# A decoder block on one Trainium2 core: every large product by tokens, turned back through DVE and DRAM

## The chip, the cores and the metric

The kernel runs on one core of a Trainium2 chip. TensorE (PE) multiplies matrices and writes PSUM; VectorE (DVE) and ScalarE (ACT) do elementwise work; GpSimd is called POOL in the profile, and SyncE (SP) issues most of the DMAs. The metric is device time in microseconds for one execution, lower is better. Before the change it was 2222.48 us (median of three runs, 2220.45 to 2222.61).

## What is computed

One layer of a decoder block on 256 tokens of width 2048, in float32:

```python
h = h + 0.5 * swiglu(rms_norm(h, ffn1_norm), ffn1_w_gate, ffn1_w_up, ffn1_w_down)   # 2048 -> 5632 -> 2048
n = rms_norm(h, mix_norm)
rq, rk, rv, rg, sq, sk, sv = split(n @ w_in)
ret = silu(rg) * groupnorm(retention(rope(rq), rope(rk), rv))     # 8 heads of 128
swa = sliding_window_attention(rope(sq), rope(sk), sv, sinks)     # 16 heads of 64, window 128
h = h + concat(ret, swa) @ w_out
h = h + cross_attention(rms_norm(h, xa_norm), rms_norm(mem, mem_norm), xa_wq, xa_wkv, xa_wo)
h = h + 0.5 * swiglu(rms_norm(h, ffn2_norm), ffn2_w_gate, ffn2_w_up, ffn2_w_down)
return rms_norm(h, final_norm)
```

## The kernel before

**Operands in two parts.** Every large product is made in a float32 form of the PE that takes operands as a high and a low part: `halves` (L70) copies the high part on ACT and subtracts it on DVE to get the low part. Three matmuls, high by high, high by low and low by high, add up to one product. Weights come in pieces of 128x1024 floats, two pieces (1 MB) a DMA on SP's queue, into three buffers `wf`; `split` (L163) makes `wh` and `wl` from each, with four buffers of each. A piece is one **step** of the program: 12 matmuls of 512 columns.

**Two forms of product.** `by_tokens` (L224) holds the activations still and streams 512 columns of weights; the result stands with tokens on the partitions. `by_weights` (L235) holds a 128x128 piece of the weights still and streams the activations: one matmul of 512 columns takes high and low parts of all 256 tokens side by side (L243), one of 256 columns adds the low part of the weights (L251). Its result is turned, with features on the partitions, as the next product wants its input. The gate and up products, the sliding-window, value and gate projections, `xa_wv` and the last down product go by tokens; the first down product, the rotary queries and keys (`w_in_rqk`), `w_out`, `xa_wk`, `xa_wq` and `xa_wo` go by weights (`turned=True`).

**The stream.** `run_stream` (L188) goes through the steps of all `Unit`s in one list. At each step it first runs the small tasks that are due (`later(n, f)` puts f n steps ahead), then emits the split of the piece three steps ahead (`LOOKAHEAD`), then the step's matmuls. When a unit's last step is out, its `done` reads the accumulator. The first 16 steps alternate between the first gate and the first up product. `pin` (L176) fixes program order for the first 16 steps; after them the framework's scheduler sets each engine's order.

**Turning what went by tokens.** The product of gate and up has its tokens on the partitions and must be turned. `up_done` (L446) multiplies on DVE and transposes 32x32 squares on DVE (L453) into a tile `box`; `move` (L459) brings the squares to their partitions by 16 DMAs of 32 KB from SBUF to SBUF on SP's queue, and `made` splits the result seven steps after the product. The stream h is kept turned (`hT`); before the last down product `turn_h` (L886) turns it to tokens by 32 transposes on PE (L892).

**Norms.** `Norm.block` multiplies a block of h by its gains in two parts, `Norm.stat` adds the squares up, `finish` takes the power on POOL (L376). The gains of a norm are in `blocks`, the scale per token is applied behind the product.

Of the kernel before, what the change touches and what calls it, by code (L numbers as in the profile page):

```python
# [17 lines left out]
P = 128  # L18
# [13 lines left out]
WARM = 12  # L32
FIRST = 16
SWA_EVERY = 5
# [3 lines left out]
def decoder_block(ctx: ExitStack, tc: tile.TileContext, a: dict, out: bass.AP):  # L38
# [5 lines left out]
    small = ctx.enter_context(tc.tile_pool(name="small", bufs=8))  # L44
    ps_acc = ctx.enter_context(tc.tile_pool(name="ps_acc", bufs=2, space=bass.MemoryType.PSUM))
# [36 lines left out]

    nc.scalar.dma_start(gains, a["gains"])
# [8 lines left out]

# [36 lines left out]
    class Unit:  # L129
# [4 lines left out]
        def __init__(self, w, index, n, lhs, done, blocks, turned=False, per_half=False, pair=False):  # L134
            self.w, self.n, self.lhs, self.done = w[2 * index : 2 * index + 2] if pair else w[index], n, lhs, done
            self.blocks, self.turned, self.per_half, self.pair = list(blocks), turned, per_half, pair
            units.append(self)
# [10 lines left out]

    def load(w, piece, count):
# [4 lines left out]
    def load_pair(w, piece, cuts=(0, 1024)):  # L154

        wf = wpool.tile([P, 2, 1024], F32, tag="wf", name=nm("wf"), bufs=3)
        src = w[:, piece].rearrange("f p n -> p f n")
        for lo, hi in zip(cuts, cuts[1:]):
            nc.sync.dma_start(wf[:, :, lo:hi], src[:, :, lo:hi])
# [3 lines left out]
    def split(wf, n, parts):  # L163
        wh, wl = (wpool.tile([P, 1024], F32R, tag=x, name=nm(x)) for x in ("wh", "wl"))
        if len(wf.shape) == 4:
            dst = [x.rearrange("p (k f n) -> p k f n", k=2, f=2) for x in (wh, wl)]
            for i in range(parts):
                ks = slice(i * 2 // parts, (i + 1) * 2 // parts)
                halves(dst[0][:, ks], dst[1][:, ks], wf[:, ks])
        else:  # L170
# [5 lines left out]
    def pin():  # L176

        prev = {}
        for ins in nc.cur_bb.bb.instructions:
            if ins.engine in prev:  # L180
# [7 lines left out]
    def run_stream():  # L188
        steps = [x for u in units for x in u.steps()]
        steps[:FIRST] = [x for y in zip(steps[: FIRST // 2], steps[FIRST // 2 : FIRST]) for x in y]  # L190
        loaded = []
        for i in range(0, FIRST, 4):
            cuts = (0, 512, 1024) if i == 0 else (0, 1024)
            for lo, hi in zip(cuts, cuts[1:]):
                load_x(i // 4, lo // S, hi // S)
                if i == 0:
                    if lo == 0:
                        wf = wpool.tile([P, 2, 1024], F32, tag="wf", name=nm("wf"), bufs=3)
                        src = steps[0][0].w[:, steps[0][3]].rearrange("f p n -> p f n")
                    nc.sync.dma_start(wf[:, :, lo:hi], src[:, :, lo:hi])  # L200
            if i == 0:
                v = wf.rearrange("p f (k n) -> p k f n", n=S)
                both = [[v[:, 2 * j : 2 * j + 2] for j in range(2)]]
            else:
                both = [load_pair(steps[i][0].w, steps[i][3])]
            both.append(load_pair(steps[i + 1][0].w, steps[i + 1][3]))
# [4 lines left out]
        def prepare(upto):  # L211
            while nxt[0] < min(upto, len(steps)):
# [8 lines left out]
                ready[at] = split(loaded[at], steps[at][0].n, 2 if at == 0 else 1)  # L221
# [10 lines left out]

        wide_first = [True]

        def by_weights(acc, x, wh, wl, first, last):  # L235

            wide = first or (wide_first[0] and not last)
            wide_first[0] = not wide

            def main_pass(closing):  # L240
                for k in range(4):
                    for f in range(2):
                        nc.tensor.matmul(  # L243
                            acc[:, f, :], wh[:, k, f * P : (f + 1) * P], x[:, k, :, :],
                            start=first and k == 0, stop=closing and k == 3,
                        )

            def low_pass():
                for k in range(4):
                    for f in range(2):  # L250
                        nc.tensor.matmul(  # L251
                            acc[:, f, :S], wl[:, k, f * P : (f + 1) * P], x[:, k, 0, :], start=False, stop=False
                        )
            if wide:
                main_pass(False)
                low_pass()
            else:
                low_pass()
                main_pass(last)

        held = []
        for at, (u, b, ks, _, first, last) in enumerate(steps):
# [16 lines left out]
            if u.turned:  # L279
                by_weights(u.acc[0], x, wh, wl, first, last)  # L280
# [16 lines left out]
        run_until(lambda: not tasks)  # L297

# [30 lines left out]
    class Norm:  # L329
# [12 lines left out]
        def block(self, b, src):  # L342

            x = blk()
            k = 0
# [3 lines left out]
            self.blocks[b] = x  # L349
# [44 lines left out]
        def scale_turned(self, x):  # L394
# [4 lines left out]
    def total(acc):  # L399

        x = t2k().rearrange("p (f s) -> p f s", f=2)
        copy(x, acc[:, :, S:])
        nc.vector.tensor_tensor(x, acc[:, :, :S], x, ALU.add)  # L403
        return x
# [8 lines left out]
    def add_to_h(j, acc, factor):  # L413

        v = hT[j // 2][:, 2 * (j % 2) : 2 * (j % 2) + 2, :]
        x = t2k().rearrange("p (f s) -> p f s", f=2)
        copy(x, acc[:, :, S:], scale=factor)
        nc.vector.tensor_tensor(v, v, x, ALU.add)  # L418
        nc.vector.scalar_tensor_tensor(v, acc[:, :, :S], factor, v, ALU.mult, ALU.add)  # L419

    def to_h(w, lhs, factor, blocks, norm=None, then=None):

        def done(acc, j):
            add_to_h(j, acc, factor)
            if norm is not None and j % 2 == 1:
# [610 lines left out]
```

## Time and profile before

| | |
|---|---|
| profiled execution | 2222.29 us |
| its span in the trace | 2220.5 us |
| mean granted PE clock | 0.997 |
| DMA | 427.04 MB, 192 GB/s on average |
| POOL | 17 instructions, no DMA |

The page gives the busy time of each engine as a share of the span; groups of instructions (line, engine, operation, what it writes and reads, count, busy time, mean of one, idle time before it and who ended it); the chain of work that ended last; and the DMAs with the time from issue to landing. The matmuls of PE are pipelined and their ends are modelled, so the spacing of their starts is what counts. Under 20 us of the span are outside PE's matmuls before the first and behind the last of the products: the first product's matmul starts at 7.60 us, and the last stores are issued from 2209.8 us on.

### The profile page before, as it was taken

Reading aid. Unit: us, or ns where it says so; the run is one execution under the profiler, and the core shown is the slowest. Engines: PE = TensorE matmul, PEld = TensorE weight load, DVE = VectorE, ACT = ScalarE, POOL = GpSimd, SP = SyncE. Lnnn points to the kernel's source line nnn. Section 1 sums busy time; section 2 is a strip of 40 time slices with the busy share of each in tenths; the row PEclk is TensorE's granted clock in tenths of the full one; section 3 lists DMA queues with packets and bytes.
Section 4 is the critical chain, followed back from the end, with each engine's and each line's share of the span. In section 5 each row is a group of like instructions: output and inputs, shape, how many; then the busy total and the mean of one; then the engine's idle time right before and its main releaser. Section 6 shows DMA issues by size and latency. Waiting matters only on the chain.

```text
span 2220.5 us, 27264 instructions
## 1 busy us (share of the span) xinstructions
PE 2199.1 (99%) x10898; PEld 1865.5 (84%) x10898; DVE 1290.8 (58%) x1540; ACT 1035.7 (47%) x1281; POOL 10.3 (0%) x17
## 2 busy tenths in 40 slices
PE   8999999999999999999999999999999999999998
PEld 7788888888888888888888889888888888888886
DVE  5555555455456678886765656664555554555554
ACT  5444434444445565555544554454444433444443
POOL 0000000000000000000000000000000000000000
PEclk9999999999999999999999999999999999999999
DMA  6556555565565554445555544454665565466563
GB/s 241 199 196 224 205 190 181 191 213 185 202 222 197 182 178 163 153 170 190 209 185 191 193 171 152 154 190 163 226 206 186 214 211 195 161 234 208 200 230 133
DMA packets 126527, 427.04 MB, mean 192 GB/s; under 512 B 12608, under 2 KB 23872, under 8 KB 126272
## 3 DMA queue, kind: packets, MB, share of 16 engines
q1 hardware_dynamic: 126256, 425.26, 55.2%
q8 instruction: 85, 1.39, 0.2%
q14 instruction: 42, 0.34, 0.0%
q10 hardware_dynamic: 144, 0.05, 0.0%
HBM read 411.62 MB, written 2.10 MB: 186 GB/s over the span
## 4 chain that ended last, share of the span: by engine, by line
PE 96%; SPq 1%; DMA 1%; DVE 1%; issue 1%; ACT 0%; ACTq 0%; POOLq 0%; POOL 0%
PE acc L410 21%; PE acc L409 21%; PE acc L408 21%; PE acc L243 20%; PE acc L251 10%; SPq L462 1%; DMA wf<-in_ffn_w_up 1%; PE tmp L408 0%; PE tmp L410 0%; PE tmp L409 0%; PE tmp L568 0%; DVE wl L73 0%; PE tmp L594 0%; ACT wh L68 0%; PE tmp L371 0%
## 5 line engine op out<-in xcount | busy, mean ns | idle before, releaser
L73 DVE TENSOR_TENSOR wl<-wf,wh 128x1024 fp32r<-128x1024 f32 (+1 forms) x773 | 936.8, 1221 | 721.0 <-ACT wh L68 715.0
L68 ACT ACTIVATE wh<-wf 128x1024 fp32r<-128x1024 f32 (+1 forms) x773 | 813.2, 1059 | 913.0 <-PE acc L410 609.7
L408 PE MATMUL acc<-wh,blk 128*128 128x512 f32 (+1 forms) x2112 | 821.0, 389 | 4.8 <-ACT wh L68 3.1
L409 PE MATMUL acc<-wl,blk 128*128 128x512 f32 (+1 forms) x2112 | 819.6, 388 | 2.2 <-DVE wl L73 2.2
L410 PE MATMUL acc<-wh,blk 128*128 128x512 f32 (+1 forms) x2112 | 819.4, 388 | 0.1
L243 PE MATMUL acc<-blk,wh 128*128 128x512 f32 x1984 | 480.8, 392 | 0.6 <-ACT wh L68 0.6
L408 PEld LDWEIGHTS acc<-wh,blk 128*128 128x128 f32 x2112 | 396.9, 188 | 86.1 <-ACT wh L68 3.9
L409 PEld LDWEIGHTS acc<-wl,blk 128*128 128x128 f32 x2112 | 397.1, 188 | 84.0 <-DVE wl L73 3.2
L410 PEld LDWEIGHTS acc<-wh,blk 128*128 128x128 f32 x2112 | 397.0, 188 | 81.9 <-DVE blk L327 0.5
L243 PEld LDWEIGHTS acc<-blk,wh 128*128 128x128 f32 x1984 | 364.3, 189 | 70.6 <-ACT wh L68 1.0
L251 PEld LDWEIGHTS acc<-blk,wl 128*128 128x128 f32 x1984 | 257.5, 192 | 15.1 <-ACT blk L68 4.9
L251 PE MATMUL acc<-blk,wl 128*128 128x256 f32 x1984 | 263.5, 284 | 3.8 <-ACT blk L68 3.8
L68 ACT ACTIVATE t2k<-acc 128x512 f32<-128x512 f32 x56 | 33.5, 598 | 126.0 <-PE acc L243 126.0
L418 DVE TENSOR_TENSOR h<-h,t2k 128x512 f32<-128x512 f32 x32 | 22.2, 693 | 53.7 <-ACT t2k L68 53.7
L73 DVE TENSOR_TENSOR blk<-blk,blk 128x512 fp32r<-128x512 f32 x44 | 28.5, 689 | 39.7 <-ACT blk L68 39.7
L68 ACT ACTIVATE blk<-blk 128x512 fp32r<-128x512 f32 x44 | 25.4, 625 | 52.2 <-DMA blk<-blk 52.2
L68 ACT ACTIVATE blk<-tmp 128x512 fp32r<-128x512 f32 (+3 forms) x57 | 26.0, 470 | 26.9 <-DVE blk L73 15.9
L452 DVE SCALAR_TENSOR_TENSOR t2k<-acc,n,t2k 128x512 f32<-128x512 f32 x44 | 31.1, 746 | 8.5 <-PE acc L410 8.5
L403 DVE TENSOR_TENSOR t2k<-acc,t2k 128x512 f32<-128x512 f32 x24 | 16.6, 690 | 32.9 <-ACT t2k L68 32.9
L443 ACT ACTIVATE t2k<-acc,n 128x512 f32<-128x512 f32 x44 | 27.6, 680 | 3.6 <-PE acc L410 3.3
L68 ACT ACTIVATE blk<-h,gains 128x256 fp32r<-128x256 f32 x64 | 28.2, 499 | 1.6 <-DVE h L419 1.6
L453 DVE STREAM_TRANSPOSE blk<-t2k 128x512 f32<-128x512 f32 x44 | 28.6, 686 | 0.0
(130 smaller groups left out, 612.1 us busy)
## 6 DMA issues: line engine op xcount, KB each, us to landing
wf<-in_ffn_w_up SPq DMA_DIRECT2D x88, 1024.0 KB, 5.4
wf<-in_ffn_w_gate SPq DMA_DIRECT2D x87, 1024.0 KB, 5.2
wf<-in_ffn_w_down SPq DMA_DIRECT2D x84, 1024.0 KB, 4.9
wf<-in_w_in_rqk SPq DMA_DIRECT2D x16, 1024.0 KB, 4.9
wf<-in_w_in_rvg SPq DMA_DIRECT2D x16, 1024.0 KB, 4.9
wf<-in_w_out SPq DMA_DIRECT2D x16, 1024.0 KB, 4.9
wf<-in_xa_wk SPq DMA_DIRECT2D x16, 1024.0 KB, 4.9
wf<-in_xa_wv SPq DMA_DIRECT2D x16, 1024.0 KB, 4.9
```

What stands on the lines that cost most here:

```text
L68: return nc.scalar.activation(dst, src, AF.Copy, **kw)
L73: nc.vector.tensor_tensor(lo, src, hi, ALU.subtract)
L243: nc.tensor.matmul(acc[:, f, :], wh[:, k, f * P : (f + 1) * P], x[:, k, :, :], start=first and k == 0, stop=closing and k == 3,)
L251: nc.tensor.matmul(acc[:, f, :S], wl[:, k, f * P : (f + 1) * P], x[:, k, 0, :], start=False, stop=False)
L408: nc.tensor.matmul(o, ah, bh, start=start, stop=False)
L409: nc.tensor.matmul(o, ah, bl, start=False, stop=False)
L410: nc.tensor.matmul(o, al, bh, start=False, stop=stop)
L418: nc.vector.tensor_tensor(v, v, x, ALU.add)
L443: nc.scalar.activation(gated[b][t], acc[:, t, :], AF.Silu, scale=norm.scale(t))
L452: nc.vector.scalar_tensor_tensor(s[t], acc[:, t, :], norm.scale(t), s[t], ALU.mult, ALU.mult)
L453: nc.vector.transpose(squares[:, :, :, t, :], s[t].rearrange("p (q b j) -> p q b j", q=4, b=4))
L462: nc.sync.dma_start(box[32 * j : 32 * j + 32, 1, i, :], box[32 * i : 32 * i + 32, 0, j, :])
```

## The change

All products that went by weights go by tokens, with 512 columns of weights and pairs of pieces (`pair=True`). What must be turned goes through the new function `cross`: DVE transposes the 32x32 squares of each half of the tokens into a tile `sq`; Pool's queue writes `sq` to a DRAM tile `box` (256 KB) and reads it back in four DMAs of 64 KB, each for 32 partitions, into `dst`; `TURN` = 4 steps later the task `then` uses the result. This takes the place of the SBUF moves of the FFNs, of the by-weights form, and of the PE transposes of h. `together` lays two units side by side, so that the steps on the last block of both stand behind all their others; it is used for the first two projections of the mixing stage, the first two `xa_wo` products and the first gate and up of FFN2. The first loads are cut smaller and begin with half a row block of gate, up's first half comes before gate's second, the first 128 KB of x come on ACT's queue, and 9 warming matmuls are issued in place of 12. At the end `pin` fixes program order for SP, ACT, DVE and POOL over the whole program.

```diff
-WARM = 12
+WARM = 9
+TURN = 4
...
+    nc.scalar.dma_start(hT[0][:, :1, :], a["x"][:P, :1, :])
     nc.scalar.dma_start(gains, a["gains"])
...
+    def all_steps():
+        out = []
+        rest = list(units)
+        while rest:
+            u = rest.pop(0)
+            x = u.steps()
+            if u.then is None:
+                out += x
+            else:
+                y = rest.pop(0).steps()
+                nx, ny = (sum(z[1] == s[-1][1] for z in s) for s in (x, y))
+                out += x[:-nx] + y[:-ny] + x[-nx:] + y[-ny:]
+        return out
...
+                src = [x[0].w[:, x[3]].rearrange("f p n -> p f n") for x in steps[:2]]
+                for j, lo, hi in ((0, 0, S), (0, S, 2 * S), (1, 0, 2 * S), (0, 2 * S, 1024), (1, 2 * S, 1024)):
+                    if j == 0 and lo > 0:
+                        load_x(0, lo // S, hi // S)
+                    nc.sync.dma_start(dst[j][:, :, lo:hi], src[j][:, :, lo:hi])
...
-        def by_weights(acc, x, wh, wl, first, last):
...
         run_until(lambda: not tasks)
+        pin([mybir.EngineType.SP, mybir.EngineType.Activation, mybir.EngineType.DVE, mybir.EngineType.Pool])
...
+    def cross(src, then, delay=TURN):
+        out = []
+        for v in src:
+            sq, dst = t2k(), t2k()
+            nc.vector.transpose(sq.rearrange("p (g q j) -> p q g j", g=4, q=4), v)
+            box = dram.tile([P, 512], F32, tag="box", name=nm("box"))
+            nc.gpsimd.dma_start(box, sq)
+            far = box.rearrange("(i r) (g n) -> g r i n", i=4, g=4)
+            for g in range(4):
+                nc.gpsimd.dma_start(dst[32 * g : 32 * g + 32, :].rearrange("p (i n) -> p i n", i=4), far[g])
+            out.append(dst.rearrange("p (i q j) -> p q i j", i=4, q=4))
+        later(delay, lambda: then(out))
+
+    def halves_of(out, x):
+        for t in range(2):
+            hi, lo = (x[:, :, c, t * P : (t + 1) * P].rearrange("p q (a j) -> p q a j", a=4) for c in range(2))
+            halves(hi, lo, out[t])
         return x
...
     def to_h(w, lhs, factor, blocks, norm=None, then=None):
-        def done(acc, j):
-            add_to_h(j, acc, factor)
...
-        for j in range(8):
-            Unit(w, j, 256, lhs, lambda acc, j=j: done(acc, j), blocks, turned=True)
+        def done(acc, b):
+            def add(out):
+                for t in range(2):
+                    v = hT[b][:, :, t * P : (t + 1) * P].rearrange("p q (a j) -> p q a j", a=4)
+                    nc.vector.tensor_tensor(v, v, out[t], ALU.add)
+                if norm is not None:
+                    norm.block(b, [hT[b]])
+                    norm.stat([hT[b]])
+                if then is not None:
+                    then(b)
+            s = [acc[:, t, :] for t in range(2)]
+            if factor != 1.0:
+                for t in range(2):
+                    s[t] = t2k()
+                    copy(s[t], acc[:, t, :], scale=factor)
+            cross([squares_of(x) for x in s], add)
+        for b in range(4):
+            Unit(w, b, 512, lhs, lambda acc, b=b: done(acc, b), blocks, pair=True)
...
-                for i in range(4):
-                    later(2 + i, lambda i=i: move(box, i))
-                later(7, lambda: made(b, box))
+                def made(out):
+                    acts[b] = halves_of(out, blk())
+                cross([squares_of(x) for x in s], made)
...
     def turn_h(b):
-        tp = [tmp_ps() for _ in range(2)]
-        for t in range(2):
-            for k in range(4):
-                nc.tensor.transpose(tp[t][:, k * P : (k + 1) * P], hT[b][:, k, t * P : (t + 1) * P], ident)
-            copy(h[t][:, b * 512 : (b + 1) * 512], tp[t])
+        def made(out):
+            for t in range(2):
+                copy(squares_of(h[t][:, b * 512 : (b + 1) * 512]), out[t])
+        cross([hT[b][:, :, t * P : (t + 1) * P].rearrange("p q (a j) -> p q a j", a=4) for t in range(2)], made)
```

`rqk_done` and `put_done` (rotary queries and keys; keys and queries of the cross-attention) change in the same way: what they did with the turned accumulator stands in a task of `cross`.

On DVE, behind the second up product of FFN1 (`t2k_644` and `t2k_645` are its products by gate, `wl` the low parts of weight pieces, `blk_927` the block for the down product), before:

```order
L453 STREAM_TRANSPOSE blk_787<-t2k_644 128x4x4x32
L453 STREAM_TRANSPOSE blk_787<-t2k_645 128x4x4x32
L73 TENSOR_TENSOR wl_793<-wf_769,wh_792 128x1024
L73 TENSOR_TENSOR wl_812<-wf_809,wh_811 128x1024
L73 TENSOR_TENSOR wl_832<-wf_809,wh_831 128x1024
L73 TENSOR_TENSOR wl_854<-wf_851,wh_853 128x1024
L73 TENSOR_TENSOR wl_874<-wf_851,wh_873 128x1024
L73 TENSOR_TENSOR blk_927<-blk_787,blk_927 128x4x128 x2
```

and now, at the same place (`t2k_791` and `t2k_800` are read back from DRAM):

```order
L417 STREAM_TRANSPOSE t2k_790<-t2k_645 128x4x4x32
L417 STREAM_TRANSPOSE t2k_799<-t2k_646 128x4x4x32
L75 TENSOR_TENSOR wl_809<-wf_770,wh_808 128x1024
L75 TENSOR_TENSOR wl_828<-wf_825,wh_827 128x1024
L75 TENSOR_TENSOR wl_844<-wf_825,wh_843 128x1024
L75 TENSOR_TENSOR wl_862<-wf_859,wh_861 128x1024
L75 TENSOR_TENSOR blk_877<-t2k_791,blk_877 128x4x128
L75 TENSOR_TENSOR blk_877<-t2k_800,blk_877 128x4x128
L75 TENSOR_TENSOR wl_883<-wf_859,wh_882 128x1024
```

Four splits stand between the transposes and the use of the result, where there were five; the split behind it, `wl_883`, cannot pass it.

On POOL, from the first norm on, before (the powers of the norms and of the group norm):

```order
L376 TENSOR_TENSOR n_105<-ms_430,mhalf 128x2
L376 TENSOR_TENSOR nmix<-ms_5610,mhalf 128x2
L720 TENSOR_TENSOR gnr_6894<-gnv_6895,mhalf 128x4
L720 TENSOR_TENSOR gnr_6936<-gnv_6937,mhalf 128x4
L720 TENSOR_TENSOR gnr_7917<-gnv_7918,mhalf 128x4
```

and now (two round trips, each of two halves):

```order
L382 TENSOR_TENSOR n_105<-ms_432,mhalf 128x2
L419 DMA box_478<-t2k_475 128x512
L422 DMA t2k_476<-box_478 32x4x128 x4
L419 DMA box_487<-t2k_484 128x512
L422 DMA t2k_485<-box_487 32x4x128 x4
L419 DMA box_793<-t2k_790 128x512
```

A write, its four reads, the second write and its four reads stand in one row; POOL has 540 DMAs where it had none, and the powers stand among them.

On ACT at the start of FFN2 (`n_109` is its norm, `blk_12201` and `blk_12202` hold h by tokens), before:

```order
L68 ACTIVATE blk_12201<-tmp_12203 128x512
L68 ACTIVATE blk_12202<-tmp_12204 128x512
L68 ACTIVATE wh_12233<-wf_12231 128x1024
L443 ACT_TABLE_LOAD
L443 ACTIVATE t2k_12249<-acc_12094,n_109 128x512
L443 ACTIVATE t2k_12250<-acc_12094,n_109 128x512
L68 ACTIVATE wh_12253<-wf_12231 128x1024
```

and now (`blk_11619` and `blk_11620` hold h by tokens, `blk_11874` is the first block for the down product):

```order
L70 ACTIVATE blk_11619<-t2k_11622 128x512
L70 ACTIVATE blk_11620<-t2k_11631 128x512
L70 ACTIVATE wh_11731<-wf_11689 128x1024
L70 ACTIVATE wh_11749<-wf_11747 128x1024
L70 ACTIVATE wh_11785<-wf_11747 128x1024
L70 ACTIVATE wh_11804<-wf_11802 128x1024
L70 ACTIVATE blk_11619<-t2k_11712 128x512
L70 ACTIVATE blk_11620<-t2k_11721 128x512
L70 ACTIVATE wh_11840<-wf_11802 128x1024
L70 ACTIVATE wh_11858<-wf_11856 128x1024
L70 ACTIVATE blk_11874<-t2k_11768 128x4x128
L70 ACTIVATE blk_11874<-t2k_11777 128x4x128
```

The copies of h came out of PSUM; now each pair stands behind a round trip through DRAM, and the first up product's trip falls among those of h.

More of the change, by code (lines that the diff above doesn't have):

```diff
@@ L342, in block, with some @@
         def block(self, b, src):
-            x = blk()
-            k = 0
+            self.some(b, src, 0)
+        def some(self, b, src, k):
+            if b not in self.blocks:
+                self.blocks[b] = blk()
+            x = self.blocks[b]
             for v in src:
@@ L348, in block @@
                 k += v.shape[1]
-            self.blocks[b] = x
         def stat(self, src):
@@ L477, in ffn @@
                 Unit(w_up, b, 512, norm.blocks, up_done(b), range(4), pair=True)
+                if b == 0 and norm is not n1:
+                    together()
             down(g, acts, fbs)
@@ L780, in decoder_block, with put_done @@
     to_h(a["w_out"], mixT, 1.0, (2, 3, 0, 1), None, out_done)
-    def put_done(norm, dst, i, f, then=None):
+    def put_done(norm, dst, i, then=None):
         def done(acc):
-            s = total(acc)
-            def finish():
-                norm.scale_turned(s)
-                if f == 0:
-                    dst[i] = blk()
-                fs = slice(2 * f, 2 * f + 2)
-                halves(dst[i][:, fs, 0, :], dst[i][:, fs, 1, :], s)
-                if f == 1 and then is not None:
+            s = [scaled(acc, t, 512, norm) for t in range(2)]
+            def made(out):
+                dst[i] = halves_of(out, blk())
+                if then is not None:
                     later(1, then)
-            later(1, finish)
+            cross([squares_of(x) for x in s], made)
         return done
@@ L812, in decoder_block @@
     for i in range(4):
-        for f in range(2):
-            Unit(a["xa_wk"], 2 * i + f, 256, nmem.blocks, put_done(nmem, keys, i, f), range(4), turned=True)
+        Unit(a["xa_wk"], i, 512, nmem.blocks, put_done(nmem, keys, i), range(4), pair=True)
     for i in range(4):
```

183 lines of the change are left out of this document (71 added, 112 removed).

## The prediction

> **What bounds the kernel now.** I read the page first: shares of the engines, then the chain that ended last.
>
> ```profile
> span 2220.5 us, 27264 instructions
> PE 2199.1 (99%) x10898; PEld 1865.5 (84%) x10898; DVE 1290.8 (58%) x1540; ACT 1035.7 (47%) x1281; POOL 10.3 (0%) x17
> PE 96%; SPq 1%; DMA 1%; DVE 1%; issue 1%; ACT 0%; ACTq 0%; POOLq 0%; POOL 0%
> ```
>
> PE is nearly always occupied, and the chain runs through it for 96%. PE's waits, from the view of who waited for whom (us in total, times, longest), are small:
>
> ```profile
> PE acc L251 <- ACT blk L68: 3.8, 2, 2.5
> PE acc L408 <- ACT wh L68: 3.1, 2, 2.2
> PE acc L409 <- DVE wl L73: 2.2, 3, 0.8
> PE acc L408 <- ACT blk L68: 1.7, 1, 1.7
> ```
>
> So the time is the number of matmuls times their spacing. Only three things can move it: the spacing, the matmuls that go, and waits that the change puts on PE. A busy PE doesn't say how fast it goes, so the spacing comes from the chain in order of time: first the old form in the first down product (start, us, what), then the form by tokens in the gate and up products.
>
> ```profile
> 301.41 1.91 PE acc L251 x16
> 303.32 3.65 PE acc L243 x16
> ...
> 412.74 1.91 PE acc L251 x16
> 149.96 0.23 PE acc L410
> ...
> 165.83 0.23 PE acc L408
> ```
>
> From 301.41 to 412.74 lie 20 periods of 16 wide and 16 narrow matmuls: 5.567 us each, 347.9 ns a pair. From 149.96 to 165.83 lie 70 matmuls of the form by tokens: 226.7 ns each.
>
> **Term A, the spacing.** The counts are in the groups by form:
>
> ```profile
> L243 PE MATMUL acc<-blk,wh 128*128 128x512 f32 x1984 | 480.8, 392 | 0.6 <-ACT wh L68 0.6
> L251 PE MATMUL acc<-blk,wl 128*128 128x256 f32 x1984 | 263.5, 284 | 3.8 <-ACT blk L68 3.8
> L892 PE MATMUL tmp<-ident,h 128*128 128x128 f32 x32 | 4.1, 272 | 0.0
> ```
>
> One pair serves one 128x128 piece of weights for all 256 tokens. By tokens, six matmuls of 512 columns serve four such pieces, so 1.5 x 226.7 = 340.1 ns a piece. 1984 x (347.9 - 340.1) = **15.5 us** less.
>
> The Trainium skill, "TensorE: Matmul & The Clock Gate", section "Wait — 56ns, not 53.3ns?", puts a warm matmul at N/2.4 + 2.5 ns. By that a pair would be 325.0 ns, the form by tokens 323.8 ns, and the term only 2.4 us. The rows disagree with it by 11 to 13 ns a matmul in both forms, and I take the rows.
>
> **Term B, the transposes of h** (L892) leave PE: 32, busy 4.1 us: **4.1 us** less. Their copies stay on ACT.
>
> **Term C, the start.** Rows of the timeline (start, us):
>
> ```profile
> 5.99 1.15 ACT L68 ACTIVATE wh<-wf 128x512 fp32r<-128x512 f32 x2 [3.54 <-DMA wf<-in_ffn_w_gate]
> 12.02 1.06 ACT L68 ACTIVATE wh<-wf 128x1024 fp32r<-128x1024 f32 x1 [3.27 <-DMA wf<-in_ffn_w_up]
> 12.98 1.14 ACT L356 ACTIVATE t2k<-h 128x512 f32<-128x512 f32 x2
> 13.13 0.50 PE L408 MATMUL acc<-wh,blk 128*128 128x512 f32 x1 [2.18 <-ACT wh L68]
> 18.62 0.40 PE L408 MATMUL acc<-wh,blk 128*128 128x512 f32 x1
> ```
>
> The matmul at 18.62 is the 25th, so PE stands as if it had started at 18.62 - 24 x 0.227 = 13.2. At 5.99 the loads had brought 768 KB, at 12.02 2560 KB: 297 KB/us. Now the first half of up's weights is the 1280th KB, there at 7.7, split at 8.8. The next limits are up's weights for block 1 (5120 KB, 20.6, split 21.7, wanted five steps of 12 x 0.227 = 2.72 us after the start): as if started at 8.1. That gains 5.1; by gate's weights for block 1 alone (4096 KB, 17.2, split 18.3, wanted after four steps) it would be 5.8. Bounds 0 (nothing that PE needs first comes later than before) and 6; I take **4 us**, near the worked-out end.
>
> **Term D, the round trip.** 54 outputs (22 up, 16 down/out products, 4 rotary, 8 keys and queries, 4 of h) each go through two 32x32 transposes on DVE, two writes of 256 KB and eight reads of 64 KB from Pool's queue. Pool holds one order: write, four reads that wait for it, write, four reads. The large products read the result nine steps later or more (only six trips, two rotary and four of queries, feed small products after five steps, 13.6 us). But ACT and DVE are in program order, and the splits of the weights stand behind the wait. So the question is how long ACT may stand still.
>
> ```profile
> ACT wh L68 <- PE acc L410: 609.7, 383, 3.5
> ACT blk L68 <- DMA blk<-blk: 52.2, 21, 4.4
> 2198.72 1.06 ACT L68 ACTIVATE wh<-wf 128x1024 fp32r<-128x1024 f32 x1 [1.66 <-PE acc L410]
> 2199.82 1.23 DVE L73 TENSOR_TENSOR wl<-wf,wh 128x1024 fp32r<-128x1024 f32 x1 [1.49 <-ACT wh L68]
> 2201.44 1.06 ACT L68 ACTIVATE wh<-wf 128x1024 fp32r<-128x1024 f32 x1 [1.66 <-PE acc L410]
> ```
>
> ACT idles 1.66 us of each 2.72 us step, for a buffer that PE frees; a split takes 2.3 us and is used three steps after it can start. The second row proves the cover: ACT already stood 21 times for moved data, up to 4.4 us, and PE lists nothing for it. Count from the end of an up product: ACT meets the halves after three steps and a split, at 9.2. The split behind them is used seven steps after the end, at 19.0. After the data come the half on ACT, then a split: 0.63 + 1.06 + 1.22 = 2.9. **The cover is 16.1 us.**
>
> What the trip takes, by the nearest rows:
>
> ```profile
> L452 DVE SCALAR_TENSOR_TENSOR t2k<-acc,n,t2k 128x512 f32<-128x512 f32 x44 | 31.1, 746 | 8.5 <-PE acc L410 8.5
> L453 DVE STREAM_TRANSPOSE blk<-t2k 128x512 f32<-128x512 f32 x44 | 28.6, 686 | 0.0
> L68 ACT ACTIVATE blk<-blk 128x512 fp32r<-128x512 f32 x44 | 25.4, 625 | 52.2 <-DMA blk<-blk 52.2
> L73 DVE TENSOR_TENSOR wl<-wf,wh 128x1024 fp32r<-128x1024 f32 (+1 forms) x773 | 936.8, 1221 | 721.0 <-ACT wh L68 715.0
> blk<-blk SPq DMA_DIRECT2D x352, 32.0 KB, 1.8
> out<-t2k SPq DMA_DIRECT2D x8, 256.0 KB, 2.5
> t2k<-in_mem SPq DMA_DIRECT2D x8, 256.0 KB, 5.7
> L462 SPq DMA_DIRECT2D blk<-blk x352: 507/589/1650, 64.8 to 2115.5; - x176
> ```
>
> Two products and a transpose on DVE, 2.2; the write 2.5 (the stores of out); four issues of 0.59 (median of L462), 2.4; the second write 2.5; three more issues, 1.8; the last read lands in 1.8 (the moves): **13.2 us**, 2.9 inside the cover. Pool's queue issued nothing before, so its price isn't shown. Low end: issues of 0.51 (the fastest of L462), 12.6. High end: every landing like the memory's load, 5.7: 23.5, or 7.4 us of wait 54 times; but those loads stood behind weight loads on SP's own queue, which is why I take the near rows.
>
> The Trainium skill, "DMA: Bandwidth & Descriptors", section "Anatomy of one DMA — SWDGE (gpsimd) path", gives 2.0 us plus bytes over 436 GB/s for one DMA of this kind; my estimate from it is 2.6 and 2.15 us, and the trip would be 13.7: also inside.
>
> Some places are tighter. Where a norm follows (8 times), ACT and DVE also do the add, four gains and two squares before the split:
>
> ```profile
> L418 DVE TENSOR_TENSOR h<-h,t2k 128x512 f32<-128x512 f32 x32 | 22.2, 693 | 53.7 <-ACT t2k L68 53.7
> L68 ACT ACTIVATE blk<-h,gains 128x256 fp32r<-128x256 f32 x64 | 28.2, 499 | 1.6 <-DVE h L419 1.6
> ```
>
> 0.69 + 4 x 0.50 + 2 x 0.57 + 2.3 = 6.1, so a cover of 12.9 against a trip of 12.3 (the first transpose starts 0.9 earlier): just enough, as it is for the six trips with 13.6. And where trips follow fast, Pool's queue, occupied 2 x (2.5 + 2.4) = 9.8 us for one, delays the next. The first two xa_wo products end two steps (5.4 us) apart: the second trip has some 16.0 against 12.9, 3 us late. At the start of FFN2 five trips start in 12 steps (33 us) and need 49: the fourth comes some 4 us late. Bounds 0 (PE's buffers absorb it) and 20; I take **7 us** more.
>
> **Program order** for ACT, DVE, Pool and SP: in the mixing stage DVE is the fullest engine:
>
> ```profile
> 743.00:1006.00 263.00, 262.57 (x1455) 227.25 (x1454) 207.64 (x402) 140.87 (x241) 3.82 (x5) 1.00 0.48 169
> ```
>
> 207.6 of 263 us (third busy column). Each of 12 window groups now blocks DVE for ACT's exponentials; 55 us of idle DVE and three steps of lookahead cover it. I take 0; bounds -1 and 10.
>
> **The sum.** The profiled execution took 2222.29 us (span 2220.5 and 1.8 around it), 0.2 below the median. 2222.3 - 15.5 - 4.1 - 4 + 7 = **2206 us**.
>
> **The rivals.**
> - *Pool's queue is slower than SP's.* The trip has seven issues in a row behind the first write, so it grows by 7 us for each us of issue. For: no row shows its speed. Against: 2.9 us of cover, and SP's 0.59 as the only row. It decides from about 0.85 us an issue, where late norm trips (8 x 1.2) and the crowded places (16) eat the gain. At 1.0 us: norm trips 8 x 2.3 = 18, crowded places 20: 2222.3 - 23.6 + 38 = 2237. At 1.25 us the up trips are 1.7 late too (37), the other 20 trips 16, norm 32, crowded 30: 2314. **Slower.** Chance 0.20. (The same page of the Trainium skill, "Specifications", has a first byte of about 1 us for DMAs from this engine against 0.6 for SP's; no run here shows it. If each issue held the queue that long, this is the case.)
> - *Program order makes PE wait*, 1 us in each of 12 window groups and 4 attentions: 2206 + 16 = 2222, **no change**. For: 79% DVE. Against: no such wait of PE before. Chance 0.08.
> - *The form by tokens gains little* here, since weights now come from the activations' side; A shrinks to 2.4: 2206 + 13 = 2219, **no change**. Against: the same form runs at 226.7 ns for two thirds of the kernel. Chance 0.04.
>
> **How the numbers follow.** The forecast, 2194 to 2218 (D from 0 to 17, C from 0 to 6), has 0.68. The range runs from 2194 up into the slow queue, 2255; left out are about 0.13 above and 0.05 below. A measurement tells 0.2%, 4.4 us, from no change. Faster: the forecast and a little of the second rival, 0.70. Same: the rest of the second, the third, and the slow queue near its threshold, 0.11. Slower: 0.19.
>
> **What would show it.** Right: no L243/L251 form; spacing of 227 ns in the down products; first up matmul near 9; ACT's waits on the read-back of 4 us at most, and PE's waits a few us, all at xa_wo and the start of FFN2. Wrong: POOLq issues of 0.9 us and more, landings above 3, and PE waits on ACT wh or DVE wl in every unit.

## The result, and the profile after

The changed kernel takes 2388.97 us (median of four executions, 2386.31 to 2393.06) against 2221.47 us in the same rounds: **1.0756 times the time before**, 95% interval 1.0737 to 1.0774, where 2206 us had been forecast. The page after, and behind it the granted clock (before: 0.997). The last number of the two DMA rows is the median time from issue to landing, in us:

```profile
span 2390.9 us, 25823 instructions
PE 2250.2 (94%) x9868; PEld 1842.2 (77%) x9868; DVE 1297.4 (54%) x1532; ACT 1014.9 (42%) x1257; POOL 310.4 (13%) x557
PE 61%; issue 14%; DMA 13%; POOL 5%; DVE 4%; ACT 4%; ACTq 0%; SPq 0%; POOLq 0%; DVEq 0%
box<-t2k POOLq DMA_DIRECT2D x108, 256.0 KB, 3.9
t2k<-box POOLq DMA_DIRECT2D x432, 64.0 KB, 3.1
core 0: 2390.9 us, clock 0.969
```

The chain that ended last ran through PE for 96% before and does for 61% now; the writes and reads of the DRAM trip and Pool's issues stand in it. Who waited for whom (us in total, times, longest), PE first, then the engines that PE waited for:

```profile
PE acc L434 <- ACT wh L70: 74.8, 28, 13.9
PE acc L435 <- DVE wl L75: 30.5, 36, 6.9
PE tmp L434 <- ACT blk L70: 10.8, 6, 4.1
ACT blk L70 <- DMA t2k<-box: 258.9, 65, 8.3
POOL t2k L422 <- DMA box<-t2k: 254.7, 60, 8.9
DVE h L445 <- DMA t2k<-box: 59.6, 16, 5.8
ACT wh L70 <- DMA wf<-in_w_out: 27.3, 6, 12.1
SPq L782 <- DMA box<-t2k: 25.2, 3, 13.0
```

Read the first six rows from the bottom: the read-back lands late, ACT stands 259 us for it in the middle of its program (52 us before), the splits of the weights stand behind, and PE runs out of split weights. All waits of PE add up to 131 us (13 before). The last two rows show a second thing that came late: SP's loads of `mem` (L782) stand for writes to DRAM, two loads of w_out behind them in program order are issued at 1113.90 and 1114.38, 18.5 us after the one before them, and ACT stands 8.0 and 2.4 us for these two.

By stages, taken from DVE's 44 products of gate and up (L452 before, L477 now): up to the last one of FFN1 the profiled execution falls only 3 us behind. From there to the first one of FFN2, through the mixing stage and the cross-attention, it takes 1003 us instead of 902, with 72 of PE's 131 us of waits. From the first to the third up product of FFN2 it takes 119 us instead of 88, and from there to the end 36 us more than before. So six tenths of the loss of 170 us lie between the two FFNs.

One late trip, in FFN2 (start, us, what, idle time before): Pool, ACT, PE.

```profile
1898.90 0.56 POOL L419 DMA_DIRECT2D box<-t2k  x1 [31.48 <-DVE t2k L417]
1903.78 2.18 POOL L422 DMA_DIRECT2D t2k<-box  x4 [4.32 <-ACT wh L70]
1905.95 0.56 POOL L419 DMA_DIRECT2D box<-t2k  x1
1914.06 2.18 POOL L422 DMA_DIRECT2D t2k<-box  x4 [7.54 <-DMA box<-t2k]
...
1912.59 0.63 ACT L70 ACTIVATE blk<-t2k 128x512 fp32r<-128x512 f32 x1 [6.79 <-DMA t2k<-box]
1917.95 0.63 ACT L70 ACTIVATE blk<-t2k 128x512 fp32r<-128x512 f32 x1 [4.73 <-DMA t2k<-box]
1918.49 3.88 ACT L70 ACTIVATE wh<-wf 128x1024 fp32r<-128x1024 f32 x4
...
1919.58 0.79 PE L434 MATMUL acc<-wh,blk 128*128 128x512 f32 x1 [4.00 <-ACT wh L70]
1920.84 0.79 PE L435 MATMUL acc<-wl,blk 128*128 128x512 f32 x1 [0.47 <-DVE wl L75]
1921.43 0.63 PE L436 MATMUL acc<-wh,blk 128*128 128x512 f32 x1
1921.86 0.63 PE L434 MATMUL acc<-wh,blk 128*128 128x512 f32 x1
...
1925.70 0.39 PE L434 MATMUL acc<-wh,blk 128*128 128x512 f32 x1
1925.93 0.40 PE L435 MATMUL acc<-wl,blk 128*128 128x512 f32 x1
1919.50:1923.00 3.50, 2.95 (x6) 2.06 (x7) 3.44 (x4) 2.87 (x4) 0.00 (x0) 0.50 0.25 50
```

The issues are cheap: 2.18 us for four, 0.55 each. But from the end of the first write's issue to the first read lie 4.3 us (the row names ACT as the one that ended this wait, but the write had landed only 0.8 us before the read), and for the second write 7.5. The second half reached ACT at 1917.95, some 21 us after the product; 2.9 us of half and split still had to come, and PE stood 4.0 and 0.5 us. The last rows show what the forecast had no term for: behind the wait matmuls start every 0.43 us instead of 0.23 until 1925.70, and the window over the first of them has a granted clock of 0.50 (the third number from the end of the last row).

### The profile page after: what moved, and what is told of

Its sections match the earlier page's. It is cut to its first block, busy times and chain, and to the rows that moved or that the text cites. A ratio compares the mean times of both kernels' runs of the same rounds, so it can differ in the third digit from the quotient of the medians.

```text
span 2390.9 us, 25823 instructions
## 1 busy us (share of the span) xinstructions
PE 2250.2 (94%) x9868; PEld 1842.2 (77%) x9868; DVE 1297.4 (54%) x1532; ACT 1014.9 (42%) x1257; POOL 310.4 (13%) x557
## 4 chain that ended last, share of the span: by engine, by line
PE 61%; issue 14%; DMA 13%; POOL 5%; DVE 4%; ACT 4%; ACTq 0%; SPq 0%; POOLq 0%; DVEq 0%
PE acc L435 20%; PE acc L436 20%; PE acc L434 19%; DMA box<-t2k 8%; POOL t2k L422 5%; DMA t2k<-box 4%; ACT wh L70 2%; DVE wl L75 2%; ACT blk L70 1%; PE tmp L436 0%; PE tmp L434 0%; PE tmp L435 0%; DMA h<-in_x 0%; ACT t2k L598 0%; DMA wf<-in_w_out 0%
## 5 line engine op out<-in xcount | busy, mean ns | idle before, releaser
L434 PE MATMUL acc<-wh,blk 128*128 128x512 f32 (+1 forms) x3104 | 1229.7, 396 | 75.3 <-ACT wh L70 74.8
L435 PE MATMUL acc<-wl,blk 128*128 128x512 f32 (+1 forms) x3104 | 1228.8, 396 | 30.6 <-DVE wl L75 30.5
L436 PE MATMUL acc<-wh,blk 128*128 128x512 f32 (+1 forms) x3104 | 1220.6, 393 | 0.0
L434 PEld LDWEIGHTS acc<-wh,blk 128*128 128x128 f32 x3104 | 593.9, 191 | 211.5 <-ACT wh L70 88.7
L435 PEld LDWEIGHTS acc<-wl,blk 128*128 128x128 f32 x3104 | 594.0, 191 | 167.2 <-DVE wl L75 45.9
L436 PEld LDWEIGHTS acc<-wh,blk 128*128 128x128 f32 x3104 | 593.9, 191 | 122.2
L422 POOL DMA_DIRECT2D t2k<-box x432 | 235.7, 552 | 429.1 <-DMA box<-t2k 254.7
L419 POOL DMA_DIRECT2D box<-t2k x108 | 61.2, 567 | 1386.6 <-DVE t2k L417 1384.4
L75 DVE TENSOR_TENSOR blk<-t2k,blk 128x512 fp32r<-128x512 f32 (+1 forms) x66 | 44.8, 680 | 213.7 <-ACT blk L70 213.7
L70 ACT ACTIVATE blk<-t2k 128x512 fp32r<-128x512 f32 (+2 forms) x74 | 46.1, 623 | 268.9 <-DMA t2k<-box 258.9
L417 DVE STREAM_TRANSPOSE t2k<-t2k 128x512 f32<-128x512 f32 x76 | 49.4, 688 | 13.4 <-ACT t2k L70 13.4
L477 DVE SCALAR_TENSOR_TENSOR t2k<-acc,n,t2k 128x512 f32<-128x512 f32 x44 | 31.0, 747 | 8.0 <-PE acc L436 8.0
L329 DVE SCALAR_TENSOR_TENSOR blk<-h,gains,blk 128x256 fp32r<-128x256 f32 x64 | 27.0, 482 | 8.2 <-ACT blk L70 8.2
```

The costliest lines, as they stand in the source:

```text
L70: return nc.scalar.activation(dst, src, AF.Copy, **kw)
L75: nc.vector.tensor_tensor(lo, src, hi, ALU.subtract)
L329: nc.vector.scalar_tensor_tensor(x[:, k, 1, :], v[:, k, :], g, x[:, k, 0, :], ALU.mult, ALU.subtract)
L417: nc.vector.transpose(sq.rearrange("p (g q j) -> p q g j", g=4, q=4), v)
L419: nc.gpsimd.dma_start(box, sq)
L422: nc.gpsimd.dma_start(dst[32 * g : 32 * g + 32, :].rearrange("p (i n) -> p i n", i=4), far[g])
```

## The experiments

Three theories stood at the start. **Theory 1**: the trip is longer than the cover, ACT and DVE stand in program order in front of it, PE waits, and the clock falls behind each wait. **Theory 2**: program order is a cause by itself. **Theory 3**: the form by tokens or its traffic slows PE by itself.

**1. Three more steps of delay (turn7).**

```diff
-TURN = 4
+TURN = 7
```

> Only the delay between a turn's reads and the instructions that use them grows, from 4 steps of the stream to 7; every instruction, every DMA and its queue stay. Theory 1 (the trip through DRAM takes 17 to 21 us, ACT and DVE stand in front of it in program order, PE runs out of split weights and its clock falls behind each wait): the cover grows by 3 x 2.72 = 8.2 us, from 16 to 24, so the late trips of the up units vanish; PE's waits fall from about 131 us to under 60 (the norm places and the start of FFN2 remain), the granted clock goes back above 0.985, 2210 to 2280 us. Theory 2 (program order by itself makes the engines wait, whatever the delay): waits on ACT and DVE hardly change, 2350 to 2390. Theory 3 (the form by tokens or the extra traffic slows PE or its clock by itself): the waits vanish but the clock stays near 0.969 and the matmul spacing above 227 ns, 2260 to 2300.

Measured: 2294.29 us, ratio 1.0338 (1.0314 to 1.0362). The late trips of the up units are gone: between 20 and 768 us and behind 1659 us PE has no wait above 1 us. Granted clock and waits:

```profile
core 0: 2292.9 us, clock 0.983
PE acc L434 <- ACT wh L70: 31.3, 11, 5.8
PE acc L435 <- DVE wl L75: 11.9, 18, 1.3
```

That is 95 us by delay alone, so most of the loss is lateness. But it is 14 us above theory 1's range, and PE's waits are 70 us where under 60 were expected. What is left stands at the norms, at the start of FFN2, and in the mixing stage, which took 299 us (from the first load of its weights to the first of `w_out`), against 263 before and 307 in the changed kernel.

**2. The scheduler's order (no_pin).**

```diff
-        pin([mybir.EngineType.SP, mybir.EngineType.Activation, mybir.EngineType.DVE, mybir.EngineType.Pool])
+        pin([])
```

> The last order is left out: ACT, DVE, Pool and SP go in the scheduler's own order from step 16 on, as before. Delay 4, queue and products stay. Theory 1: the scheduler may put splits ahead of the halves that wait for a late read-back, so a part of the waits goes, 2300 to 2370; where its order is the same, nothing changes. Theory 2 (program order is the cause): nearly all waits go, 2200 to 2225, clock 0.997. Theory 3: no change, 2380 to 2395.

Measured: 2261.29 us, 1.0177 (1.0152 to 1.0203): below the range of theory 1 and above that of theory 2. With the order free, ACT still stood 203 us for read-backs, yet splits went ahead of halves that waited, and PE's waits fell to 51.5 us. Both remedies work on the same loss, by two ways.

**3. Both writes first (writes_first).**

```diff
-            sq, dst = t2k(), t2k()
+            sq = t2k()
...
             nc.gpsimd.dma_start(box, sq)
+            boxes.append(box)
+        for box in boxes:
+            dst = t2k()
```

> In each turn both writes to DRAM are issued on Pool's queue ahead of all eight reads (before: write, four reads, write, four reads). Delay 4. Theory 1: the second write no longer waits for the first write's landing and for four reads, and it lands beside the first instead of behind the reads (5.0 us there, 3.1 for the first); the trip falls from 16.7 to some 12 to 14 us, the cover holds again in the up units: PE's waits under 60 us, clock above 0.985, 2205 to 2290 us. Theory 2 and 3: the order on Pool's queue matters little, 2370 to 2390.

Measured: 2290.25 us, 1.0318 (1.0303 to 1.0333), at the edge of theory 1's range; PE's waits are 71 us, where under 60 were expected. The writes land sooner, but the eight reads, now together, later:

```profile
box<-t2k POOLq DMA_DIRECT2D x108, 256.0 KB, 2.9
t2k<-box POOLq DMA_DIRECT2D x432, 64.0 KB, 5.0
```

From the issue of the first write to the last landing a trip took 13.8 us in the median (14.5 in the changed kernel), and the longest 16.9 (20.0). So the median trip hardly changed, and the time fell by 99 us.

**4. h turned by PE (turnh_pe)**: the four lines of `turn_h` as before the change.

> The four turns of h at the start of FFN2 go back to TensorE transposes (32 transposes of 128x128, about 4 us) and leave Pool's queue: 46 to 50 turns stay. Prices the crowd at the start of FFN2, where PE lost about 45 us between 1600 and 1740 us. Theory 1: that loss falls to what one late turn costs elsewhere (2 to 4 us in each unit), so 30 to 45 us less, 2345 to 2362. Theory 2 and 3: about +4 us for the transposes, 2388 to 2395.

Measured: 2332.77 us, 1.0514 (1.0496 to 1.0533): 56 us less, more than the 30 to 45 of theory 1, for 4 us of transposes. The forecast had 7 us for all crowded places together. But not all of it lies at the start of FFN2. The two profiled executions differ by 60 us: 30 of them from FFN2's first to its third up product (89 us instead of 119), 6 ahead of that and 24 behind it, where the edit changes nothing; why PE waited less there isn't shown.

**5. No weight loads (no_weights).** Why do the landings take 3.9 and 3.1 us, where 2.5 and 1.8 had been taken?

```diff
+        if len(kept) < 6:
+            kept.append(wpool.tile([P, 2, 1024], F32, tag="wf", name=nm("wf"), bufs=3))
+            nc.sync.dma_start(kept[-1], w[:, piece].rearrange("f p n -> p f n"))
+        wf = kept[-1]
```

> From step 16 of the stream on no weights are loaded: every split reads the last tile that was loaded (so all later products use wrong weights; every instruction of PE, ACT, DVE and Pool stays, and all of Pool's DMAs). It asks why the landings on Pool's queue came out longer than forecast (3.9 and 3.1 us, not 2.5 and 1.8). Theory 1a (they share the DMA engines with the weight loads; in the changed kernel's own rows a write beside no weight load took 2.3 and a read 2.2): medians fall to 2.3 to 2.6 and 2.1 to 2.4, the trip to about 14 us, inside the cover; PE's waits under 50 us (norms and the start of FFN2 remain), 2210 to 2260 us. Theory 1b (Pool's queue is slow by itself): medians stay above 3.5 and 2.8, 2340 to 2390.

Measured: 2239.88 us, 1.009 (1.0069 to 1.011). Without the weights, DMA moved 33 GB/s. Pool's part of the traffic (q0: packets, MB, share of the 16 DMA engines' span), its landings and PE's waits:

```profile
HBM read 43.57 MB, written 30.41 MB: 33 GB/s over the span
q0 software_dynamic: 22464, 56.66, 7.4%
box<-t2k POOLq DMA_DIRECT2D x108, 256.0 KB, 2.4
t2k<-box POOLq DMA_DIRECT2D x432, 64.0 KB, 2.2
PE acc L437 <- ACT wh L70: 19.9, 12, 6.2
PE acc L438 <- DVE wl L75: 7.9, 11, 0.8
```

So theory 1a holds. The landings forecast were those of a queue that has the DMA engines to itself; beside the weight loads the same transfers take 1.6 and 1.4 times as long, and leaving the loads out is worth 2389 - 2240 = 149 us. The row of q0 reads the same on the changed kernel's page, 7.4% of 2390.9 us there and of 2237.0 here: the packets' own time is some 7% longer there, the landing of a write 60%. That speaks for packets that stand in line, more than for packets that are slower. By stages, 84 of the 101 us lost between the FFNs come back, 24 of the 31 at the start of FFN2, and 33 of the 36 behind it. (The experiment also frees ACT from waits for weights, 33 us in the changed kernel, 27 of them for `w_out`; a part of the 149 may be that.)

**6. Program order alone, in the kernel before (before_pin).**

> The kernel before, with the last order alone added: ACT, DVE, Pool and SP in program order to the end. Theory 1 (program order only hurts where a moved result comes late): the moves of before land in time, PE's waits grow by at most 10 us, in the mixing stage; 2219 to 2240. Theory 2 (program order is a cause by itself): 2260 to 2350.

Measured: 2260.65 us, 1.0182 (1.0165 to 1.0199), the low edge of theory 2. The mixing stage took 284 us instead of 263; most of the other 19 us lie in the FFNs, where SP, with its moves (L464) in program order, stands for DVE's transposes and weight loads come late. Before, then with the order:

```profile
SPq L462 <- DVE blk L453: 116.1, 22, 6.3
ACT wh L68 <- DMA wf<-in_ffn_w_gate: 3.5, 1, 3.5
```

```profile
SPq L464 <- DVE blk L455: 241.5, 22, 12.0
ACT wh L68 <- DMA wf<-in_ffn_w_gate: 125.5, 17, 8.8
```

So theory 2 holds as well, for 40 us, without any trip through DRAM. The part of the moves can't be carried over to the changed kernel, which has none.

**7. The trip from SP's queue (sp_queue)**: delay 7, the writes as tasks one step after the product, the reads after three, on SP.

> The changed kernel with delay 7, and the trips through DRAM issued from SP's queue, which carries the weight loads too: the writes one step after the product, the reads after three. To be compared with delay 7 alone (2294). Theory 1a (what hurts is sharing the DMA engines with the weight loads of another queue): in one queue the transfers stand in line, landings near 2 to 3 us once reached, and the result comes no later than step 7; but SP stands until a write has landed before it can issue reads and further weight loads: 2260 to 2300. Rival (SP's standing makes the weight loads late): waits on DMA of wf appear, 2300 to 2400.

Measured: 2315.27 us, 1.0434 (1.0411 to 1.0458): the rival. One queue doesn't save the trip, because SP in program order stands for the transposes and the weight loads stand behind it:

```profile
SPq L420 <- DVE t2k L417: 747.9, 104, 23.0
ACT wh L70 <- DMA wf<-in_ffn_w_gate: 230.0, 44, 10.1
```

It doesn't say what SP's queue would cost with the order free.

**8. to 11. The remedies together.** All three (combo), and then each pair, complete the table of delay, order and who turns h.

> Three remedies together on the changed kernel: delay 7, the scheduler's order from step 16 on, h turned by PE. Theory 1: the late trips of the up units are gone, as are the crowd at the start of FFN2 and the splits behind late halves; what is left are the waits for the norms (3 to 7 us each, four places) and the start: PE's waits 20 to 35 us, clock 0.990 or more, 2222 to 2245 us. If the gain of the form by tokens (19.6 us) is real and all waits could go, the floor is 2203 + 4. Theory 3 (the form costs by itself): 2250 or more although the waits are gone.

> Delay 7 and the scheduler's order, with the turns of h through DRAM as changed: the three remedies together (2210) less the one for h. Theory 1: the four turns of h crowd Pool's queue at the start of FFN2 only; with free splits and delay 7 that crowd costs 5 to 25 us: 2214 to 2235. If h's turns cost through DRAM whatever the order (56 us, as at delay 4 in program order): 2260 or more.

> Delay 7 and h turned by PE, with ACT, DVE, Pool and SP in program order as changed: the three remedies less the scheduler's order. Theory 1 with program order as a cost of its own (40 us in the kernel before, with nothing else changed): 2210 + 35 to 50 = 2245 to 2262. If program order only hurts by way of late results (theory 1 as first put): 2215 to 2235.

> Delay 4, the scheduler's order and h turned by PE: the three remedies less the delay. Theory 1: the scheduler's order is made by its own idea of landing times, so late halves still stand ahead of splits in the later units; without the crowd of h the loss of the scheduler's order alone (2261) shrinks by 20 to 35 us: 2225 to 2245.

| delay | order | h turned | time, us | ratio to before (95%) |
|---|---|---|---|---|
| 4 | program | DRAM | 2388.97 | 1.0756 (1.0737 to 1.0774) |
| 7 | program | DRAM | 2294.29 | 1.0338 (1.0314 to 1.0362) |
| 4 | scheduler | DRAM | 2261.29 | 1.0177 (1.0152 to 1.0203) |
| 4 | program | PE | 2332.77 | 1.0514 (1.0496 to 1.0533) |
| 7 | scheduler | DRAM | 2229.68 | 1.0039 (1.0024 to 1.0053) |
| 7 | program | PE | 2269.33 | 1.0213 (1.0195 to 1.0231) |
| 4 | scheduler | PE | 2242.03 | 1.0102 (1.0077 to 1.0128) |
| 7 | scheduler | PE | 2210.27 | 0.9955 (0.994 to 0.997) |

With the other two in place, each remedy is still worth something: h 19 us, delay 32, order 59 (some 6 us less each when combo's second measurement, 2216.11, is taken). turn7_turnh_pe came out 7 us above its range for program order as a cost of its own, so that cost is nearer 60 than 40 us here; 57 of it lie between the FFNs. With h on PE, that stretch took 995 us at delay 4, 952 at delay 7 and 895 in combo, with the order free as well. combo came out 12 us below its range: theory 1 had left 20 to 35 us of waits, and 14 were left. The last row beats the kernel before; theory 3 falls with it, as its waits and clock are those of before and its time is lower:

```profile
span 2207.9 us, 25810 instructions
PE 2184.0 (99%) x9900; PEld 1810.8 (82%) x9900; DVE 1286.9 (58%) x1524; ACT 1025.6 (46%) x1257; POOL 287.6 (13%) x517
box<-t2k POOLq DMA_DIRECT2D x100, 256.0 KB, 3.2
t2k<-box POOLq DMA_DIRECT2D x400, 64.0 KB, 3.4
core 0: 2207.9 us, clock 0.996
```

The trips are as slow as ever (3.2 and 3.4 us); nothing waits for them any more.

**12. The form by tokens where it is safe (cand)**: the kernel before, with the first half of FFN1's down product, `xa_wk` and `xa_wq` by tokens and through `cross` at delay 7, all else as before.

> The kernel before, with the form by tokens only in the first half of FFN1's down product, xa_wk and xa_wq (112 of the 248 steps), each with its trip through DRAM from Pool's queue at delay 7; up's moves, w_out, xa_wo, the rotary products, h, the first loads and the order stay as before. Theory 1: 112 x 8 x 7.8 ns = 7.0 us less, and no norm stands behind a trip: 2211 to 2217. If the gain by tokens is not real: 2219 to 2226.

Measured: 2215.82 us, 0.9975 (0.9965 to 0.9984), 3.6 to 7.8 us less. That is theory 1's range, and the 7.0 us of term A lie within the interval.

**13. and 14. The start (combo_head, combo_again).** In the changed kernel ACT stands for x's second half, and up's split is next in its program:

```profile
6.21 0.49 ACT L70 ACTIVATE blk<-h,gains 128x256 fp32r<-128x256 f32 x1
10.42 0.91 ACT L70 ACTIVATE blk<-h,gains 128x256 fp32r<-128x256 f32 x2 [3.72 <-DMA h<-in_x]
11.23 1.04 ACT L70 ACTIVATE wh<-wf 128x1024 fp32r<-128x1024 f32 x1
```

```diff
-            later(0, lambda: n1.some(0, [hT[0][:, 2:, :]], 2))
+            later(1, lambda: n1.some(0, [hT[0][:, 2:, :]], 2))
```

> The three remedies (2210), and the gains of x's second half move from ahead of up's first split to behind it in the code of the start. Term C was forecast at 4 us and measured 0.8 (25th product at 17.80 instead of 18.62), since ACT stood for x's second half and up's split stood behind it. If that order is the cause: up's first product goes from 12.08 to 9 to 10 us, the 25th product from 18.3 to 15 to 16.5, and the time falls by 1.5 to 3 us. If up's weights themselves land late: no change, first up product near 12.

> The three remedies once more, on the chip and in the rounds of the run before it, so that the two can be compared: 2207 to 2213, ratio to the kernel before 0.994 to 0.997.

With the edit the split leads, and it waits for its own weights:

```profile
9.78 1.06 ACT L70 ACTIVATE wh<-wf 128x1024 fp32r<-128x1024 f32 x1 [1.20 <-DMA wf<-in_ffn_w_up]
10.75 0.89 ACT L70 ACTIVATE blk<-h,gains 128x256 fp32r<-128x256 f32 x2
```

Up's first product moved from 12.08 us (combo; 11.56 in combo_again) to 10.89, and the 25th product from 17.19 (16.93; not 18.3, as the expectation has it) to 14.79: the order held up's first product by 0.7 to 1.2 us, and the rest is up's weights, which were there at 9.78 and not at the forecast 7.7. In time the two can't be told apart: 2213.55 us, 0.9968 (0.9957 to 0.998), and 2216.11 us, 0.9977 (0.9967 to 0.9987). combo_again lies above the range that was written for it; its executions run from 2208.66 to 2221.01, its interval just overlaps that of the same kernel in the table, and its profiled execution had longer waits of PE (21 us, 14 in the first). What is sure is a gain of 0.1 to 0.6% over the kernel before.

## Why the prediction was wrong, point by point

- **What bounds the kernel.** Right for the kernel before, and the spacing and the count did fall as forecast; but time as matmuls, spacing and waits lacks a factor. Granted clock times span gives it: 2390.9 x (1 - 0.969) = 74 us, against 2220.5 x (1 - 0.997) = 7 before. 118 us of new waits brought 67 us of half speed with them. 2222 - 20 + 118 + 67 = 2387, and the profiled execution took 2393.
- **Term A, 15.5 us.** Borne out. 112 of its 248 steps gave 3.6 to 7.8 us in cand, where 7.0 was due.
- **Term B, 4.1 us.** The transposes left PE. Their replacement, put under D, was worth 56 us in the wrong direction.
- **Term C, 4 us.** 0.8 in the changed kernel (25th product at 17.80, not 18.62). The bound "nothing that PE needs first comes later" held; what I left out is that x's second half stands between up's weights and PE on ACT, and up's weights landed at 9.73 us, not at 7.7.
- **Term D, the failed step.** The cover of 16.1 us was right: an FFN1 trip whose second half reached ACT 16.7 us after the product cost PE 0.34 us. The issues were even cheaper than taken (0.55 us, not 0.59). What failed is the landing: 2.5 and 1.8 us came from stores at the end of the kernel, when no weights were loading, and from moves that stood in SP's own queue. The changed DMAs share the engines with the weight loads, and take 3.9 and 3.1; alone they take 2.4 and 2.2 (no_weights), by which the sum would be 2.2 + 2.4 + 4 x 0.55 + 2.4 + 3 x 0.55 + 2.2 = 13.1 us, as forecast. With 3.9 and 3.1 it is 17.0, only 0.9 over the cover; the trips above the median are later. With the 2.2 us on DVE the 54 trips took 14.8 to 22.2 us, 16.7 in the median, and 37 of them more than 16.1, the cover of the up trips; without weight loads they took 13.4 to 18.0, 14.0 in the median. So the price fell less on the FFN1 trips, where PE's waits add up to 8 us, than between the FFNs, where norms and small products follow and the cover is shorter, and on the slow trips of FFN2. I gave the row that contradicted it, 5.7 us for a load beside weight loads, as the high end, and then put it aside because it stood behind weight loads on one queue; and I kept its price, 7.4 us of wait 54 times, out of the range.
- **Crowded places, 7 us, bounds 0 and 20.** Between the first and the third up product of FFN2 alone 31 us were lost. Taking h's trips out brought back 30 there, and 56 in all. Here too the landings make most of the crowd: Pool's queue holds each trip until its writes land, and without weight loads 24 of the 31 us come back.
- **Program order, 0 us, bounds -1 and 10.** 40 us in the kernel before (before_pin), and 59 with delay 7 and h on PE. Idle DVE in the mixing stage was no cover, since an engine in order waits with free time in hand; and SP, which I did not count at all, delays weight loads: in before_pin behind moves, in the changed kernel behind the loads of `mem`, after which ACT stood 8.0 and 2.4 us for w_out. Without weight loads (no_weights) the kernel took 2240 with the order kept, 34 us over the forecast: less than the order is worth in the other runs, so a part of its price, too, seems to hang on transfers that come late.
- **The rivals.** The slow queue came true in sign and place (late splits, in most units though not in every one), by its landings and not by its issue, for which the threshold was worked out. Program order was the second rival, with 16 us where the runs show 40 and more. The third, a form that gains little, did not hold.
- **The range.** Its ends don't follow from its terms: C from 0 to 6 and D from 0 to 17 give 2197 to 2220, not 2194 to 2218. The result lies far outside both.

The Trainium skill has the rule that decides D: "DMA: Bandwidth & Descriptors", section "Issuing engines are not separate DMA queues", says that DMAs from all issuing engines run on the same 16 DMA engines and interleave. The runs agree: 3.9 against 2.4 us for one write, with packets that themselves took some 7% longer. The fit that the prediction cited from that page, 2.6 and 2.15 us, is within 0.2 us of no_weights: a price without other traffic.

## What to carry to other kernels

A DMA's landing time belongs to the traffic beside it: price a new transfer by rows that lie beside the kernel's main stream, not by the same queue or size in a quiet place, and give a moved result several steps more than the sum says. Leave engines that prepare the next operands an order in which a late result can be passed over, or put its use late enough that it never is late; when every engine is put in program order, count the waits of each, the DMA-issuing one too. And on a kernel that keeps PE full, a wait of a few microseconds costs itself and then, often, 1.7 us or more at half clock.

## What had not been expected of the hardware

The clock falls in pieces. In the 16 traces of this case every stretch at half clock after the start lay at a pause of PE and was 3.4, 6.8, 10.2 or 17.1 us long, but for one at each program's end (5.3 to 8.9 us). Counting PE's waits above 0.25 us after the first 20 us, those less than 8 us apart as one: of 129 below 1.6 us one had a stretch at half clock at it or within 5 us behind it, of 97 between 1.6 and 3.5 us 48, of 62 above 3.5 us 60, with 6.9 us of half clock on average, so 3.5 us lost beside the wait. This is read from traces and was not tried by itself. The Trainium skill, "TensorE: Matmul & The Clock Gate", section "What's actually happening", has PE at half clock after an idle window of about 3.4 us, in windows that run free of the kernel; the lengths agree with it, but here pauses of 1.6 to 3 us were enough in 35 of 80 cases.

A wait of PE thus cost about 1.6 times its length in the changed kernel (118 us of new waits, 67 of clock).
